# A second split of the input blocks, unscaled gate and up products, and another order of high parts, in a hybrid decoder step

## The chip, the cores and the metric

The kernel runs on one core of a Trainium2 chip. The metric is the device time of one execution in microseconds (us). A core has TensorE for matrix products (PE in the profile, and PEld for the loading of the stationary operand), VectorE (DVE), ScalarE (ACT), GpSimd (POOL) and SyncE (SP), which here only issues transfers. Each engine takes its instructions in the order in which they are written, and they wait for one another by semaphores.

## The reference

One layer of a decoder for 256 prompt positions and 8 sample tokens, together T = 264 columns: a half-step SwiGLU, a mixing block of four mLSTM heads beside a gated short convolution, another half-step SwiGLU, and a last RMSNorm. What matters here:

```python
def swiglu(x, wg, wu, wd):
    return (jax.nn.silu(x @ wg) * (x @ wu)) @ wd
h = h + 0.5 * swiglu(rmsnorm(h, norm_ffn1[l]), ffn1_gate[l], ffn1_up[l], ffn1_down[l])
mix, ... = mixing_block(rmsnorm(h, norm_mix[l]), w_in[l], ..., w_out[l], ...)
h = h + mix
h = h + 0.5 * swiglu(rmsnorm(h, norm_ffn2[l]), ffn2_gate[l], ffn2_up[l], ffn2_down[l])
```

D_MODEL is 2048, D_FF 5504; everything is float32. `rmsnorm` multiplies each token by the reciprocal root of its mean square, and each channel by a gain.

## The kernel before

**Data.** Channels lie on partitions, the 264 tokens in the free dimension. 2048 channels are 16 blocks of 128; D_FF is 43 blocks, taken in two halves of 22 and 21 (blocks 0 to 21, then 22 to 42). For each half all gate and up products are made, then the down products of that half for the 16 output blocks, which are added to the residual `h`.

**Three float16 products for a float32 one.** Each float32 operand is split into a high and a low float16 part. For weights ScalarE makes the high part (`high`, L246: a scaled copy) and VectorE the low one (`low`, L254: scaled source less high part). A block product is then three matmuls, high by high, high by low and low by high (`three`, L364 to L366); the third one of a weight tile is the first that needs VectorE's low part.

**Pairs.** For some blocks ("pairs") the gate and up products, or two down products, are made together by a seven-product scheme (`product_pair`): 264-column matmuls for the high parts (L438) and 132-column matmuls for the corrections (L423, L424). It needs sums of weight parts (`weight_sums`, L339, L342, L343, on VectorE), sums of token halves (`token_sums`, L411, made once for the input of an FFN and once for every eight blocks of activations), and a join of the results (`join`, one copy on ScalarE at L476 and six operations on VectorE, L479 to L486). A block that is no pair is called plain here.

**The norm.** The RMSNorm's per-token factor is not known when the input blocks are split (the sum of squares is still being made), so the split takes the bare `h` times the gain, and every gate and up product is multiplied by the factor `norm.r` afterwards: L895 for a pair, L914 and L920 for a plain block. Then follow Silu (ScalarE), the product of the two (L863), and the split of the activation into parts (L246 and L254 again, tiles `a`).

**Weights.** `weight_plan` lists the weight tiles in their order of use; `fetch` takes the next one: SyncE issues the transfer into one of three float32 buffers (`wraw`), ScalarE makes the high part in one of four buffers (`w`), VectorE the low part, and for a tile of a pair the sums. A tile holds 16 blocks of 128 x 128 (1 MB); a pair's gate and up are two tiles of 8 + 8. Three tiles are kept ahead of the product in work (`AHEAD`). In the FFNs the low part is put off (`held`, `lag`): `fetch` is called in the middle of a product, and the low part is written at the start of the next one (`release`).

**Order.** The order on each engine is that in which the Python code runs. Work that belongs beside the products is put on an agenda: `at(n, f)` runs f at the n-th following `tick`; each product makes a full tick at its start and half a tick in its middle. The activation work of a block so runs in the ticks of the next blocks' products. All VectorE and ScalarE instructions of one tick stand in their queues before what follows in the code, the next low part for one.

**Check and second pass.** The kernel checks that sums of its products lie in bounds, and if one doesn't, a branch runs the whole step again in a float32 form. That code stands in the program and isn't executed otherwise.

## Time and profile before

| | |
|---|---|
| time, median of 3 runs | 1855.82 us (1854.87 to 1857.45) |
| profiled execution | 1855.79 us, span 1854.1 us |
| TensorE busy | 1790.9 us, 97% |
| VectorE busy | 1617.1 us, 87% |
| ScalarE busy | 864.8 us, 47% |
| read from memory | 366.72 MB |

The stages on the profile's time axis: FFN 1 from the start to about 712 us (its second half's gate and up products between about 373 and 590), the mixing block to about 1140, FFN 2 to the end. A row of the waits says which engine, tile and line waited for which, with the total, the number and the longest; a row of the timeline gives start, duration, engine, line and tiles, and in brackets how long the engine stood before it and for whom. A matmul's duration is its passage through the array; matmuls overlap, so what one costs is read from the distance of starts.

### The profile page before, as it was taken

How to read it: one execution, taken by the hardware profiler on the slowest of the kernel's cores; microseconds unless marked ns; L12 is line 12 of the kernel's file. 1: busy time of each engine (PE TensorE's matmuls, PEld its weight loads, DVE VectorE, ACT ScalarE, POOL GpSimd, SP SyncE). 2: the span in 40 equal slices, each digit the busy share in tenths (PEclk: the TensorE clock that was granted, in tenths of full speed). 3: DMA queues.
4: the chain of work that ended last, by engine and by line, in shares of the span. 5: the costliest groups of instructions: out<-in, count | busy, mean ns of one | idle time of the engine just before them, and what ended most of it. 6: DMA issues, size and time to landing. Idle time of an engine off the chain costs nothing.

```text
span 1854.1 us, 44580 instructions
## 1 busy us (share of the span) xinstructions
PE 1790.9 (97%) x19596; PEld 1600.9 (86%) x19596; DVE 1617.1 (87%) x2196; ACT 864.8 (47%) x1216; POOL 160.1 (9%) x200
## 2 busy tenths in 40 slices
PE   9999999989999999999999999999999999999997
PEld 7889988979988987888888888998888987988886
DVE  7899989999997898788887866999989999999785
ACT  7534443334444435466566644444443434444442
POOL 1000000000000222322121021000000000000241
PEclk9999999999999999999999999999999999999999
DMA  8555555555555556878777655555565655555653
GB/s 299 197 183 203 186 195 190 193 198 189 205 206 169 185 165 224 290 257 300 275 248 259 215 202 172 196 186 204 182 209 172 213 198 195 198 186 188 197 176 125
DMA packets 90794, 381.45 MB, mean 206 GB/s; under 512 B 9788, under 2 KB 19612, under 8 KB 71392
## 3 DMA queue, kind: packets, MB, share of 16 engines
q1 hardware_dynamic: 81392, 350.51, 55.4%
q0 software_dynamic: 8256, 27.57, 4.4%
q8 instruction: 155, 2.54, 0.6%
q10 hardware_dynamic: 944, 0.45, 0.1%
q14 instruction: 47, 0.39, 0.1%
HBM read 366.72 MB, written 11.78 MB: 204 GB/s over the span
## 4 chain that ended last, share of the span: by engine, by line
DVE 47%; PE 39%; issue 6%; ACT 4%; DMA 4%; POOL 1%; SPq 0%; DVEq 0%; ACTq 0%; POOLq 0%
DVE w L254 20%; PE ps L366 11%; PE ps L364 11%; PE ps L365 11%; DVE s L339 8%; DVE s L342 4%; ACT w L246 2%; DVE s L343 2%; PE ps L438 2%; PE ps L424 2%; PE ps L423 2%; DMA wraw<-in_w1d 1%; DVE y L895 1%; DVE y L480 1%; DVE a L254 1%
## 5 line engine op out<-in xcount | busy, mean ns | idle before, releaser
L254 DVE SCALAR_TENSOR_TENSOR w<-wraw,w 128x2048 f16<-128x2048 f32 (+3 forms) x351 | 753.5, 2151 | 86.3 <-ACT w L246 86.1
L246 ACT ACTIVATE w<-wraw 128x2048 f16<-128x2048 f32 (+3 forms) x351 | 620.1, 1780 | 197.2 <-DMA wraw<-in_w1d 66.3
L366 PE MATMUL ps<-x,w 128*128 128x264 f16 x1280 | 358.0, 280 | 28.5 <-DVE w L254 28.4
L366 PEld LDWEIGHTS <-w 128*128 128x128 f16 x3028 | 297.9, 98 | 85.6 <-DVE w L254 40.6
L364 PE MATMUL ps<-x,w 128*128 128x264 f16 x1280 | 357.8, 280 | 0.0
L365 PE MATMUL ps<-x,w 128*128 128x264 f16 x1280 | 357.6, 279 | 0.0
L365 PEld LDWEIGHTS <-w 128*128 128x128 f16 x3028 | 298.1, 98 | 46.7
L364 PEld LDWEIGHTS <-w 128*128 128x128 f16 x3028 | 298.2, 98 | 45.3 <-issue 0.6
L364 PE MATMUL ps<-xm,w 128*128 128x264 f16 x896 | 248.1, 277 | 0.0
L366 PE MATMUL ps<-xm,w 128*128 128x264 f16 x896 | 248.1, 277 | 0.0
L365 PE MATMUL ps<-xm,w 128*128 128x264 f16 x896 | 248.1, 277 | 0.0
L438 PEld LDWEIGHTS <-w 128*128 128x128 f16 x2230 | 213.8, 98 | 29.7
L424 PEld LDWEIGHTS <-s 128*128 128x128 f16 x2216 | 215.1, 97 | 0.0
L423 PEld LDWEIGHTS <-s 128*128 128x128 f16 x2216 | 213.1, 96 | 1.8 <-DVE s L343 1.1
L339 DVE TENSOR_TENSOR s<-w 128x2048 f16<-128x2048 f16 (+2 forms) x145 | 173.1, 1194 | 7.7
L424 PEld LDWEIGHTS <-w 128*128 128x128 f16 x1676 | 163.2, 97 | 12.3 <-DVE w L254 10.0
L438 PE MATMUL ps<-x,w 128*128 128x264 f16 x1408 | 172.8, 276 | 0.0
L423 PEld LDWEIGHTS <-w 128*128 128x128 f16 x1676 | 163.2, 97 | 2.3
L366 PE MATMUL ps<-a,w 128*128 128x264 f16 (+2 forms) x596 | 156.8, 270 | 5.7 <-DVE w L254 5.7
L364 PE MATMUL ps<-a,w 128*128 128x264 f16 (+2 forms) x596 | 156.7, 270 | 0.0
L365 PE MATMUL ps<-a,w 128*128 128x264 f16 (+2 forms) x596 | 156.7, 269 | 0.0
L423 PE MATMUL ps<-f,s 128*128 128x132 f16 x1056 | 130.8, 220 | 0.0
(276 smaller groups left out, 2582.1 us busy)
## 6 DMA issues: line engine op xcount, KB each, us to landing
wraw<-in_w2gu SPq DMA_DIRECT2D x86, 1024.0 KB, 5.1
wraw<-in_w1gu SPq DMA_DIRECT2D x82, 1024.0 KB, 5.2
wraw<-in_win SPq DMA_DIRECT2D x56, 1024.0 KB, 5.7
wraw<-in_w1d SPq DMA_DIRECT2D x20, 1024.0 KB, 5.0
wraw<-in_w2d SPq DMA_DIRECT2D x18, 1024.0 KB, 5.0
wraw<-in_wout SPq DMA_DIRECT2D x16, 1024.0 KB, 4.8
wraw<-in_w2d SPq DMA_DIRECT2D x18, 704.0 KB, 4.1
wraw<-in_w1d SPq DMA_DIRECT2D x16, 704.0 KB, 4.1
```

The source lines that it names most:

```text
L246: nc.scalar.activation(dst, src, AF.Copy, scale=scale)
L254: nc.vector.scalar_tensor_tensor(dst, src, scale, hi, op0=ALU.mult, op1=ALU.subtract)
L339: nc.vector.tensor_tensor(s[:, 0:2], bc, d_.unsqueeze(1).to_broadcast([128, 2, m, 2, 128]), op=ALU.add)
L342: nc.vector.tensor_tensor(s[:, 2], s[:, 1], b_, op=ALU.add)
L343: nc.vector.tensor_tensor(s[:, 3], s[:, 2], a_, op=ALU.add)
L364: nc.tensor.matmul(ps, wh, xk[:, 0, :], start=first, stop=False)
L365: nc.tensor.matmul(ps, wh, xk[:, 1, :], start=False, stop=False)
L366: nc.tensor.matmul(ps, wl, xk[:, 0, :], start=False, stop=last)
L423: nc.tensor.matmul(ps, w[0], x[:, 1], start=first, stop=False)
L424: nc.tensor.matmul(ps, w[1], x[:, 0], start=False, stop=last)
L438: nc.tensor.matmul(ps[:, :T], hi[:, i], xs[i][:, 0], start=(k0 + i == 0), stop=False)
L480: nc.vector.tensor_tensor(y[:, 1:3], p[:, 1:3], y[:, 4].unsqueeze(1).to_broadcast([128, 2, TH]), op=ALU.add)
```

## The change

- **Blocks split a second time.** Once `norm.r` is known, `renew` multiplies each of the 16 input blocks by gain and norm (L820 in the new numbering) and splits the result again (L249 on ScalarE, L257 on VectorE), two blocks at each half tick, over four products (blocks 3 and 4 of FFN 1, 1 and 2 of FFN 2). From block 5 (FFN 1) or 3 (FFN 2) on, the products use the new blocks (`swap`), whose token sums (`form`) are made after that.
- **Products unscaled.** From there on a product needs no multiplication by the norm: Silu reads it with a constant scale, for a plain block directly from PSUM (L950), and the product of gate and up takes the scale along (L899).
- **High parts in front.** In gate, up and down products the next tile is fetched at the product's start, ahead of the activations on the agenda for that tick, and its low part is written in the middle of the same product.
- **Small pieces in the mixing.** The weight tiles of the mixing's projections are fetched in halves of 8 blocks (512 KB), each split on its own; lookahead is counted in halves (`AHEAD` 6).
- **Pairs.** 45 gate and up pairs instead of 44, spread more evenly (never three in a row), and 17 down pairs instead of 19.
- The join has its own buffer in two copies.

```diff
+def spread(b0, b1, n):
+    return [b0 + i for i in range(b1 - b0) if (i + 1) * n // (b1 - b0) > i * n // (b1 - b0)]
 GU_SEVEN = {
-    n: [b0 + i for b0, b1 in ((first, 21), (22, NFB - 1)) for i in range(b1 - b0) if i % 5 in (0, 2, 3)]
-    for n, first in (("1", 7), ("2", 3))
+    "1": spread(7, 21, 9) + spread(22, NFB - 1, 13), "2": spread(4, 21, 10) + spread(22, NFB - 1, 13),
 }
 DOWN_SEVEN = {
-    ("1", 0): (1, 2, 3, 5, 6, 7), ("1", 1): (1, 3, 4, 6),
-    ("2", 0): (1, 2, 3, 5, 6, 7), ("2", 1): (1, 3, 4),
+    ("1", 0): (1, 3, 4, 6, 7), ("1", 1): (1, 3, 4, 6),
+    ("2", 0): (1, 3, 4, 6, 7), ("2", 1): (1, 3, 4),
 }
...
     def add(key, src, n, m=128):
-        parts = -(-n // (WIDE if sevens else WK))
+        halves = sevens and key[0] in ("in", "out")
+        parts = -(-n // (WIDE if sevens and not halves else WK))
...
-    AHEAD = 3 if half_size else 2
+    AHEAD = 6 if half_size else 2
...
+    def product_wide(key, x, order, final):
+        ps, k = bank()[:, :T], 0
+        count = len(order)
+        while k < count:
+            while room() or not ready:
+                fetch()
+            hi, lo, n = take(key)
+            if room() and not (final and k):
+                fetch()
+            if k == 0:
+                tick()
+                middle = n if n < count else n // 2
+            for i in range(n):
+                three(ps, hi[:, i], lo[:, i], x[order[k]], k == 0, k == count - 1)
+                k += 1
+                if k == middle:
+                    release()
+                    tick(0.5)
+                    middle = 0
+            release()
+        return ps
...
     def product_pair(key, x, forms, order):
-        tick()
...
         while k0 < count:
-            while plan and len(ready) + len(held) < AHEAD or not ready:
+            while room() or not ready:
                 fetch()
-            got, hi, lo, n = ready.pop(0)
-            assert got == key, (got, key)
-            release()
+            hi, lo, n = take(key)
+            if room():
+                fetch()
+            if k0 in (0, WK):
+                tick()
             s = sums.pop(0)
...
-            fetch()
+            release()
             if last or k0 == 0:
                 tick(0.5)
...
-            if k0 == n:
-                tick()
...
+        def renew(self, *blocks):
+            for kb in blocks:
+                g, i = kb // WK, kb % WK
...
+                t, x = t264("sq"), self.new[g][:, i]
+                gain = whole[:, self.col + kb : self.col + kb + 1]
+                nc.vector.scalar_tensor_tensor(t, h[kb], gain, self.r, op0=ALU.mult, op1=ALU.mult)
+                split(x, t, 1.0)
+        def swap(self):
+            self.groups, self.scaled = self.new, True
+            self.x = [t[:, i] for t in self.new for i in range(WK)]
...
+                    nc.vector.scalar_tensor_tensor(
+                        zu, src, unit, sg, op0=ALU.mult, op1=ALU.mult
+                    )
...
                 def halves():
                     rest()
-                    nc.vector.tensor_tensor(
-                        z, z, norm.r.unsqueeze(1).to_broadcast([128, 2, T]), op=ALU.mult
-                    )
-                    nc.scalar.activation(sg, z[:, 0], AF.Silu)
+                    nc.scalar.activation(sg, z[:, 0], AF.Silu, scale=unit)
...
+                    if norm.scaled:
+                        sg = t264("tb")
+                        nc.scalar.activation(sg, pg, AF.Silu, scale=unit)
+                        watch(pg, scalar=True)
+                        pu = gate_up(j, "u")
+                        activated(j, i, t264("tc"), sg, pu)
+                        watch(pu, scalar=True)
+                        return
...
+                    if half_size and j == (5 if start is not None else 3):
+                        norm.swap()
...
                     if half_size and j == (3 if start is not None else 1):
+                        for n in range(WK):
+                            at(1 + n / 2, norm.renew, 2 * n, 2 * n + 1)
                         for g in range(2):
-                            at((4 + 2 * g) if start is not None else (1 + g), norm.form, g)
+                            at(6 + g + (start is not None), norm.form, g)
```

How the order moves is shown at three places. First VectorE in FFN 1, around the end of a plain block that stands behind a pair and in front of one; `w` are weight tiles, `s` their sums, `tc` the product of gate and up, `a1` the activation's parts. Before:

```order
L920 TENSOR_TENSOR tc_2251<-ps_2198,rstd_621 128x264
L863 TENSOR_TENSOR tc_2251<-tc_2251,tb_2189 128x264
L254 SCALAR_TENSOR_TENSOR w_2224<-wraw_2223,w_2224 128x16x128
L339 TENSOR_TENSOR s_2261<-w_2224 128x2048
L342 TENSOR_TENSOR s_2261<-s_2261,w_2224 128x1024
L343 TENSOR_TENSOR s_2261<-s_2261,w_2224 128x1024
L254 SCALAR_TENSOR_TENSOR a1_1469<-y5_2116,a1_1469 128x264
L254 SCALAR_TENSOR_TENSOR a1_1469<-tc_2251,a1_1469 128x264
L254 SCALAR_TENSOR_TENSOR w_2282<-wraw_2281,w_2282 128x16x128
```

With the change, at the like place:

```order
L899 SCALAR_TENSOR_TENSOR tc_2131<-ps_2071,tb_2067 128x264
L257 SCALAR_TENSOR_TENSOR w_2140<-wraw_2139,w_2140 128x16x128
L360 TENSOR_TENSOR s_2160<-w_2140 128x2048
L363 TENSOR_TENSOR s_2160<-s_2160,w_2140 128x1024
L364 TENSOR_TENSOR s_2160<-s_2160,w_2140 128x1024
L257 SCALAR_TENSOR_TENSOR a1_1600<-y4_1997,a1_1600 128x264
L257 SCALAR_TENSOR_TENSOR a1_1600<-tc_2131,a1_1600 128x264
L257 SCALAR_TENSOR_TENSOR w_2223<-wraw_2222,w_2223 128x16x128
```

The multiplication by the norm is gone; behind the activation's product stands, as before, a low part, but of another tile, as the second place shows: ScalarE at the same stretch (`seen` is the bounds check's read). Before:

```order
L246 ACTIVATE a1_1469<-y5_2116 128x264
L246 ACTIVATE w_2224<-wraw_2223 128x16x128
L246 ACTIVATE a1_1469<-tc_2251 128x264
L647 ACTIVATE seen_2255,stat_172<-ps_2198 128x16
L246 ACTIVATE w_2282<-wraw_2281 128x16x128
L246 ACTIVATE w_2365<-wraw_2364 128x16x128
```

With the change:

```order
L249 ACTIVATE w_2073<-wraw_2072 128x16x128
L249 ACTIVATE a1_1600<-y4_1997 128x264
L249 ACTIVATE a1_1600<-tc_2131 128x264
L658 ACTIVATE seen_2134,stat_173<-ps_2071 128x16
L249 ACTIVATE w_2140<-wraw_2139 128x16x128
L249 ACTIVATE w_2223<-wraw_2222 128x16x128
```

The tile whose low part VectorE makes right behind the activation's product (w_2224, now w_2140) had its high part ahead of that activation's split; now it has it behind. Third, VectorE in FFN 2, where input blocks are split again; `sq` is a block times gain and norm, `r0` its new parts:

```order
L820 SCALAR_TENSOR_TENSOR sq_15845<-h0_80,whole_166,rstd_15727 128x264
L257 SCALAR_TENSOR_TENSOR r0_15811<-sq_15845,r0_15811 128x264
L820 SCALAR_TENSOR_TENSOR sq_15849<-h0_80,whole_166,rstd_15727 128x264
L257 SCALAR_TENSOR_TENSOR r0_15811<-sq_15849,r0_15811 128x264
L957 TENSOR_TENSOR ta_15877<-ps_15804,rstd_15727 128x264
L820 SCALAR_TENSOR_TENSOR sq_15888<-h4_81,whole_166,rstd_15727 128x264
L257 SCALAR_TENSOR_TENSOR r0_15811<-sq_15888,r0_15811 128x264
L820 SCALAR_TENSOR_TENSOR sq_15892<-h4_81,whole_166,rstd_15727 128x264
L257 SCALAR_TENSOR_TENSOR r0_15811<-sq_15892,r0_15811 128x264
L257 SCALAR_TENSOR_TENSOR w_15885<-wraw_15884,w_15885 128x16x128
```

Between two of VectorE's rows of one block lies ScalarE's high part of it; the high part of w_15885 stands on ScalarE ahead of those of h4's two blocks:

```order
L658 ACTIVATE seen_15879,stat_173<-ps_15804 128x16
L960 ACTIVATE tb_15881<-ta_15877 128x264
L249 ACTIVATE w_15885<-wraw_15884 128x16x128
L249 ACTIVATE r0_15811<-sq_15888 128x264
L249 ACTIVATE r0_15811<-sq_15892 128x264
```

Four low parts of weight tiles stand among the sixteen blocks in this way. In all the program issues 74 more weight transfers, and TensorE has 112 more matmuls of 264 columns and 196 fewer of 132.

More of the change, by code (lines that the diff above doesn't have):

```diff
@@ L135, in weight_plan @@
     half = KB // 2
-    if sevens:
-        beside(("two", 0), a["wout"][0:2], KB)
-    else:
-        for k0 in (0, half):
-            for db in range(2):
-                add(("out", db), a["wout"][db][:, k0 : k0 + half], half)
+    for k0 in (0, half):
+        for db in range(2):
+            src = a["wout"][db][:, k0 : k0 + half]
+            plan.append((("out", db), src, half, 128, 1, db if sevens else None))
     for db in range(2, KB):
@@ L263, in fetch @@
             return
-        key, src, n, m, several = plan.pop(0)
+        key, src, n, m, several, sub = plan.pop(0)
         if half_size and key == "four":
             raw, parts = small()
+        elif half_size and sub == 1:
+            raw, parts = (t[:, WK:] for t in pair)
         elif half_size:
@@ L269, in fetch @@
             parts = wpool.tile([128, WIDE, 2, 128], PART, tag="w", name="w", bufs=4)
+            pair[:] = raw, parts
             raw = raw[:, :, :m]
@@ L298, in fetch, with size, room, take @@
         release()
-        held.append((lows, (key, parts[:, :, 0], parts[:, :, 1], n), parts))
+        held.append((lows, (key, parts[:, :, 0], parts[:, :, 1], n, size(key, sub)), parts))
         if not lag[0]:
             release()
-    held, lag = [], [False]
+    held, lag, pair = [], [False], []
+    def size(key, sub):
+        return 0 if key == "four" else 2 if half_size and sub is None else 1
+    def room():
+        if not plan:
+            return False
+        asked = sum(t[4] for t in ready) + sum(t[1][4] for t in held)
+        return asked + size(plan[0][0], plan[0][5]) <= AHEAD
+    def take(key):
+        got, hi, lo, n, _ = ready.pop(0)
+        assert got == key, (got, key)
+        return hi, lo, n
     def release():
@@ L496, in product_beside @@
         ps = bank()[:, :T]
-        while plan and len(ready) + len(held) < AHEAD:
+        while room() or not ready:
             fetch()
-        got, hi, lo, n = ready.pop(0)
-        assert got == key and n == KB, (got, key, n)
+        hi, lo, n = take(key)
         for k in range(0, n, 4):
@@ L542, in products2 @@
             for j, key in enumerate(keys):
-                while plan and len(ready) + len(held) < AHEAD:
+                while room() or not ready:
                     fetch()
-                got, hi, lo, n = ready.pop(0)
-                assert got == key, (got, key)
+                hi, lo, n = take(key)
                 for i in range(n):
@@ L551, in products2 @@
                     )
-                fetch()
+                if room():
+                    fetch()
                 if j == 0:
@@ L604, in products4 @@
                     squares(i, i + 1)
-            _, hi, lo, _ = ready.pop(0)
+            hi, lo, _ = take("four")
             for n, (w, part) in enumerate(((hi, 0), (hi, 1), (lo, 0))):
@@ L872, in activated @@
                 if lag[0] and j < blocks[-1] - 2:
-                    at(0.5 if j in sevens and j + 1 in sevens else 1.5, low, *rest)
+                    at(1.5, low, *rest)
                 else:
```

103 lines of the change are left out of this document (42 added, 61 removed).

## The prediction

> **What bounds the kernel now.** I read the page's first part, then who TensorE waited for, then the stages, then VectorE's own order of time at the longest wait.
>
> ```profile
> span 1854.1 us, 44580 instructions
> PE 1790.9 (97%) x19596; PEld 1600.9 (86%) x19596; DVE 1617.1 (87%) x2196; ACT 864.8 (47%) x1216; POOL 160.1 (9%) x200
> ```
>
> TensorE leaves 63.2 us of the span. The waits of TensorE say whom it waited for (total, times, longest):
>
> ```profile
> PE ps L366 <- DVE w L254: 34.1, 21, 4.0
> PE ps L424 <- DVE w L254: 7.5, 8, 1.6
> ```
>
> So 41.6 us are the third matmul of a block, which needs the low part of a weight tile, waiting for VectorE (L254). By stages (columns: PE, PEld, DVE, ACT, POOL busy, clock, DMA share, GB/s):
>
> ```profile
> 365.00:605.00 240.00, 229.85 (x2660) 206.89 (x2658) 222.12 (x283) 103.86 (x140) 0.63 (x1) 0.99 0.57 195
> 712.00:1150.00 438.00, 431.64 (x3745) 372.55 (x3734) 335.86 (x581) 253.27 (x404) 89.33 (x132) 1.00 0.70 246
> ```
>
> In the second half of FFN 1 (365 to 605) VectorE has no room: 222 of 240 us, and the same waits there, and VectorE's own for the tiles' high parts (365 to 590), are
>
> ```profile
> PE ps L366 <- DVE w L254: 9.7, 5, 4.0
> PE ps L424 <- DVE w L254: 0.4, 1, 0.4
> ```
> ```profile
> L254 DVE SCALAR_TENSOR_TENSOR w<-wraw,w 128x2048 f16<-128x2048 f32 (+1 forms) x42 | 95.1, 2266 | 1.4 <-ACT w L246 1.4
> ```
>
> In the mixing (712 to 1150) it has 100 us of it, and no TensorE wait there names a weight tile. At the longest wait VectorE is back to back (first fence), and TensorE stands for 4 us (second):
>
> ```profile
> 400.56 2.28 DVE L254 SCALAR_TENSOR_TENSOR w<-wraw,w 128x2048 f16<-128x2048 f32 x1
> 402.94 1.23 DVE L339 TENSOR_TENSOR s<-w 128x2048 f16<-128x2048 f16 x1
> 404.20 0.69 DVE L342 TENSOR_TENSOR s<-s,w 128x1024 f16<-128x1024 f16 x1
> 404.93 0.69 DVE L343 TENSOR_TENSOR s<-s,w 128x1024 f16<-128x1024 f16 x1
> 405.54 0.28 DVE L479 TENSOR_TENSOR y<-y,ps 128x132 f32<-128x132 f32 x1
> ...
> 407.56 0.71 DVE L895 TENSOR_TENSOR y<-y,rstd 128x528 f32<-128x528 f32 x1
> 408.18 2.28 DVE L254 SCALAR_TENSOR_TENSOR w<-wraw,w 128x2048 f16<-128x2048 f32 x1
> 410.38 0.43 DVE L863 TENSOR_TENSOR y<-y,tb 128x264 f32<-128x264 f32 x1
> 410.73 2.29 DVE L254 SCALAR_TENSOR_TENSOR w<-wraw,w 128x2048 f16<-128x2048 f32 x1
> ```
> ```profile
> 410.52 0.29 PE L366 MATMUL ps<-x,w 128*128 128x264 f16 x1 [3.99 <-DVE w L254]
> ```
>
> The starts give prices on a loaded VectorE: a low part with its sums 4.98 (400.56 to 405.54), a low part alone 2.20, the join 2.02 (405.54 to 407.56), the product with the norm 0.62, a small operation 0.35. TensorE's prices:
>
> ```profile
> 1147.20:1168.80 21.60, 21.60 (x194) 18.77 (x193) 16.14 (x23) 10.77 (x18) 0.00 (x0) 1.00 0.38 120
> ```
> ```profile
> 385.18 1.96 PE L438 MATMUL ps<-x,w 128*128 128x264 f16 x16
> ...
> 390.19 0.39 PE L438 MATMUL ps<-x,w 128*128 128x264 f16 x2
> ```
>
> Four plain products take 21.60, so a plain block (gate and up) 10.80; half a pair 5.01, a pair 10.02. A pair costs VectorE 2 x 4.98 + 2.02 + 0.62 + 2 x 0.35 = 13.30, a plain block 2 x 2.20 + 4 x 0.38 = 5.9. Twelve pairs and 8 plain blocks with 7 for the token sums are 214 against 207 on TensorE: 7 short, and 10.1 are waited in that window. This account of VectorE therefore fits, and I use it for the change.
>
> **The change, part by part.** TensorE: 112 more matmuls of 264 columns and 196 fewer of 132. At 21.60/192 = 0.1125 and (5.01 - 16 x 0.1125)/56 = 0.0573 that is 12.6 - 11.2 = **+1.3 us**.
>
> Norm product gone: a pair costs VectorE 12.68, a plain block after the switch 2 x 2.20 + 2 x 0.38 = 5.2. Over 45 pairs and 33 plain blocks that is 28 + 23 = 51 us off its work, and two fewer down pairs take off about 2 x 9 more.
>
> But two things are put in front of its low parts. First, **the place of the high part**. Before, the tile fetched in the middle of the up product had its high part ahead of that block's activation; now the tile's high part stands behind it on ScalarE, and VectorE's next instruction after the activation product is this tile's low part (the two rows of VectorE's order shown above, L899 and then L257). The chain is in the trace:
>
> ```profile
> 1156.32 0.43 DVE L863 TENSOR_TENSOR tc<-tc,tb 128x264 f32<-128x264 f32 x1
> ```
> ```profile
> 1156.84 0.42 ACT L246 ACTIVATE a<-tc 128x264 f16<-128x264 f32 x1 [3.22 <-issue]
> 1157.16 0.17 ACT L647 ACTIVATE seen<-ps 128x16 f32<-128x16 f32 x1
> 1157.23 0.19 ACT L647 ACTIVATION_READ_ACCUMULATOR seen<-ps 128x1 f32 x1
> 1157.32 1.90 ACT L246 ACTIVATE w<-wraw 128x2048 f16<-128x2048 f32 x1
> ```
>
> From the product's end (1156.75) to the high part's end (1159.22) are 2.5 us in which VectorE, being in order, does nothing. A VectorE that is early doesn't mind; a late one pays 2.5 per plain block, so 7.7 instead of 5.2. Bounds: 0 and 2.5; I take 2.5, because a plain block and two pairs cost VectorE 5.2 + 25.4 = 30.6 against 30.8 on TensorE even without it: any wait makes it late. With it: 33.1 against 30.8. Thirteen pairs and 7 plain blocks are 165 + 54 + 7 = 226 against 206, 20 short. The fetch is half a product earlier than before, and by walking one cycle through the order its tightest tile is ready 6 us early; take that off, and a little for fewer pairs in a row ahead of it: **12.5 us** of waiting where 10.1 are now.
>
> Second, **the second split** (L820 and the two splitting operations): 16 blocks in each FFN, each VectorE, ScalarE, VectorE in turn. The same pattern before:
>
> ```profile
> 1141.51 0.43 DVE L1697 SCALAR_TENSOR_TENSOR h<-ps,h 128x264 f32<-128x264 f32 x1 [0.29 <-PE ps L366]
> 1142.53 0.49 DVE L254 SCALAR_TENSOR_TENSOR x<-h,gains,x 128x264 f16<-128x264 f32 x1 [0.58 <-ACT x L246]
> 1142.94 0.17 DVE L651 TENSOR_REDUCE stat<-ps 128x1 f32<-128x16 f32 x1
> ```
>
> 1.43 per block, or 1.33 with a constant scale: 21 us. Of the four blocks that share a product, the first two have a weight tile's high part ahead of them on ScalarE (third order fence): 2 more, four times: 8. All this falls into four products, 21.6 on TensorE, in which VectorE also has four low parts and some 8 small operations (12): 41 against 21.6. Walking FFN 2 with these prices from 1158.3 (where the old token sums start), the low parts of products 3 up, 4 gate and 4 up come 4.5, 4.7 and 3.2 late, the next few 2 to 3 together: **15 us**. In FFN 1 VectorE is already hard up where this begins,
>
> ```profile
> 54.43 2.28 DVE L254 SCALAR_TENSOR_TENSOR w<-wraw,w 128x2048 f16<-128x2048 f32 x1
> ```
>
> the tile done at 56.7 for a product that starts at 57.8: **18 us**. Bounds: 0 if the splits ran in VectorE's idle time, 24 with no lead at all. What is late next is the rest of the first halves, now entered without lead: 9 pairs and 4 plain blocks in FFN 1 (145 + 5 against 133, less the 6 that plain blocks 5 to 7 give back, **11**), 9 and 6 in FFN 2 (160 + 5 against 155, less 1, **9**).
>
> Down products and start: the waits now, in the down products that end FFN 1 (605 to 712) and in the first 100 us,
>
> ```profile
> PE ps L366 <- DVE w L254: 2.1, 1, 2.1
> PE ps L424 <- DVE w L254: 1.6, 1, 1.6
> ```
> ```profile
> PE ps L366 <- DVE w L254: 1.9, 1, 1.9
> ```
>
> The second-half down products keep their pairs: 3 each, **6**. The first halves lose their three pairs in a row: 0. The start keeps its **1.9**. Mixing: 72 tiles in two pieces; VectorE and ScalarE have the room (window above), SyncE's 74 more issues are free. Without that cover it would be a fixed part per piece, under 0.2 each, 14 us.
>
> The sum against the profiled run (1855.79, span 1854.1, 1.7 around it; median 1855.82, so no shift): waits for weight tiles 1.9 + 18 + 15 + 11 + 9 + 2 x 12.5 + 6 = 86 in place of 41.6, +1.3: 1855.8 + 44 + 1.3 = **1901 us**.
>
> A row for a cost beyond the wait itself, the granted clock after the 4 us wait:
>
> ```profile
> 411.00:416.00 5.00, 5.00 (x32) 3.65 (x30) 4.47 (x9) 2.34 (x3) 0.00 (x0) 0.66 0.83 282
> 416.00:421.00 5.00, 5.00 (x47) 4.34 (x46) 4.90 (x5) 2.22 (x2) 0.00 (x0) 1.00 0.62 198
> ```
>
> Fifteen matmuls fewer, about 1.7 us. While VectorE is the late one, this gives it time and costs nothing more, so it isn't in the sum. The Trainium skill, "TensorE: Matmul & The Clock Gate" (HAM oscillation), says that idle gaps above about 3.4 us bring the clock back to half; the trace agrees (0.66 in that window). By that rule alone, some six to eight such gaps would add 10 to 14 us, an estimate, and give about 1913.
>
> **The rivals.**
>
> *Faster, the waits go.* VectorE has 69 us less to do, and 32 x 0.86 = 28 more from the splits; if the waits on ScalarE fell into time in which it waits for TensorE anyhow, all but about 7 of the 41.6 would go, and with them four slow-clock stretches of 1.7: 1855.8 - 35 - 7 + 1.3 = 1815. For it: the fetch is half a product earlier, pairs never stand three in a row. Against it: the order of rows shown, and 30.6 against 30.8 without any wait.
>
> *No change.* The 2.5 is hidden, but the splits are paid: 1.9 + 18 + 15 + 5 = 40 for 41.6: 1855.
>
> *Slower by the transfers.* The mixing's 72 tiles come as two transfers. Issues and their time to landing:
>
> ```profile
> wraw<-in_w2d SPq DMA_DIRECT2D x18, 1024.0 KB, 5.0
> ...
> wraw<-in_w2d SPq DMA_DIRECT2D x18, 704.0 KB, 4.1
> ...
> raw<-in_w1gu SPq DMA_DIRECT2D x16, 256.0 KB, 5.7
> ```
> ```profile
> 0.00:25.00 25.00, 22.60 (x197) 19.42 (x198) 18.73 (x42) 17.77 (x33) 2.43 (x11) 1.00 0.96 318
> ```
>
> At 3.6 a half (estimate: 4.1 less 192 KB at the slope of the two upper rows), one after the other, 7.2 against the 5.4 that a product lasts: 72 x 1.8 = 130, 2030 with the rest. Against it: the 256 KB pieces at the start overlap and reach 318 GB/s. [...]
>
> **How the numbers follow.** Forecast 66%, faster 21%, no change 9%, transfers 4%. The forecast's own range is 1878 to 1922 (the wait terms off by a quarter, all one way). Reaching to the no-change case and a little of the faster one, and leaving the transfers out, 8 in 10 lie in **1846 to 1922**. A measurement here tells 0.2% (3.7 us) from no change: faster 0.22, same 0.08, slower 0.70.
>
> **What would show it.** Right: TensorE's waits for VectorE's low part (now L257) at 70 to 100 us in all; VectorE's waits for ScalarE's high part in the FFNs, near 2.5 us at each plain block behind a pair, where the second half of FFN 1 has 1.4 in all; waits of 3 to 6 us near 63 to 85 us and soon after FFN 2 begins; none in the mixing. Wrong: VectorE on time in the second halves, or its splits overlapping. If the unscaled products left the bounds that the kernel checks, its second, float32 pass would run and the time would more than double; I give that under 1%.

## The result and the profile after

The changed kernel takes 1912.37 us (1910.23 to 1917.14, 4 runs) where the kernel before takes 1856.51 us (the median of four runs beside it): a ratio of 1.0305, 95% interval 1.0284 to 1.0327. It is 3% slower, 56 us in the medians. The profiled executions are 1917.14 us, the longest of the four, and 1855.79 us, with spans of 1915.4 and 1854.1 us, so the profiles have 61.3 us to explain.

The first part of the page of the changed kernel:

```profile
span 1915.4 us, 44686 instructions
PE 1809.5 (94%) x19512; PEld 1605.0 (84%) x19512; DVE 1574.6 (82%) x2207; ACT 878.9 (46%) x1325; POOL 144.8 (8%) x200
```

VectorE has 42.5 us less to do than before (1617.1), as the change intends, and the kernel is longer. TensorE's waits, whole run (total, times, longest):

```profile
PE ps L387 <- DVE w L257: 50.7, 25, 4.7
PE ps L385 <- ACT r L249: 23.3, 16, 3.2
PE ps L474 <- ACT w L249: 7.2, 6, 1.8
PE ps L385 <- ACT w L249: 3.6, 3, 1.8
PE ps L458 <- DVE w L257: 3.1, 8, 0.8
```

These rows are 87.9 us; the two rows of before were 41.6. L387 and L458 are the old waits for a low part of a weight tile. The second row is new in kind: `r` are the input blocks split a second time, and TensorE waits for them one by one. The third and fourth are waits for a high part. And VectorE's largest wait, whole run, before and after:

```profile
DVE w L254 <- ACT w L246: 86.1, 59, 4.2
```
```profile
DVE w L257 <- ACT w L249: 189.4, 110, 3.9
```

In the order of the change VectorE, about to write a tile's low part, finds ScalarE's high part not there 110 times, in place of 59. Before, 63.6 of the 86.1 us lay in the mixing, where VectorE has time to spare; now 34.8 of the 189.4 do.

The stages, each from the first matmul of its kind to the first of the next kind (read from TensorE's rows of the two traces, us):

| stage | before | after | difference |
|---|---|---|---|
| start and first half gate and up, FFN 1 | 246.4 | 270.6 | +24.2 |
| down, first half | 116.4 | 118.3 | +1.9 |
| gate and up, second half | 232.4 | 231.9 | -0.5 |
| down, second half | 115.8 | 122.4 | +6.6 |
| mixing | 430.4 | 424.1 | -6.3 |
| first half gate and up, FFN 2 | 233.3 | 255.5 | +22.2 |
| down, first half | 117.1 | 118.1 | +1.0 |
| gate and up, second half | 233.2 | 232.8 | -0.4 |
| down, second half, and end | 129.2 | 141.7 | +12.5 |

Three quarters of the loss lie where the blocks are split a second time. There VectorE's and TensorE's order of time are these (FFN 1, `sq` a block times gain and norm, `r` its new parts):

```profile
85.71 0.43 DVE L257 SCALAR_TENSOR_TENSOR r<-sq,r 128x264 f16<-128x264 f32 x1 [2.42 <-ACT r L249]
86.06 0.49 DVE L820 SCALAR_TENSOR_TENSOR sq<-h,whole,rstd 128x264 f32<-128x264 f32 x1
87.04 0.43 DVE L257 SCALAR_TENSOR_TENSOR r<-sq,r 128x264 f16<-128x264 f32 x1 [0.49 <-ACT r L249]
87.39 2.28 DVE L257 SCALAR_TENSOR_TENSOR w<-wraw,w 128x2048 f16<-128x2048 f32 x1
```
```profile
85.73 0.38 PE L385 MATMUL ps<-r,w 128*128 128x264 f16 x1 [3.22 <-ACT r L249]
...
87.06 0.38 PE L385 MATMUL ps<-r,w 128*128 128x264 f16 x1 [0.26 <-ACT r L249]
...
90.58 0.38 PE L385 MATMUL ps<-r,w 128*128 128x264 f16 x1 [2.46 <-ACT r L249]
```

From one low part to the next, 85.71 to 87.04, are the 1.33 us that the prediction worked with. In front of the first stands the wait of 2.42 us behind a tile's high part. TensorE has already begun the product that uses the new blocks and goes at the pace of the split, three matmuls at a time. The last of the splits comes long after the product that needs them has begun: 28.5 us in FFN 1 (63.4 to 91.9) and 22.5 us in FFN 2 (1200.2 to 1222.7), where such a product takes 5.4 without waits.

In the second half of FFN 1 the place of the high part shows as forecast, VectorE first, ScalarE second:

```profile
409.02 0.43 DVE L899 SCALAR_TENSOR_TENSOR tc<-ps,tb 128x264 f32<-128x264 f32 x1
411.90 2.29 DVE L257 SCALAR_TENSOR_TENSOR w<-wraw,w 128x2048 f16<-128x2048 f32 x1 [2.45 <-ACT w L249]
```
```profile
409.48 0.42 ACT L249 ACTIVATE a<-tc 128x264 f16<-128x264 f32 x1 [5.84 <-DVE tc L899]
...
409.97 3.70 ACT L249 ACTIVATE w<-wraw 128x2048 f16<-128x2048 f32 x2
```

ScalarE stood still for 5.84 us, nearly all of it with the tile's data there (they had landed at 404.1), because the activation's split, which waits for the product's end, is in front of the high part.

### The profile page after: what moved, and what is told of

It reads as the page before. It is cut to its first block, busy times and chain, and to the rows that moved or that the text cites. A ratio compares the mean times of both kernels' runs of the same rounds, so it can differ in the third digit from the quotient of the medians.

```text
span 1915.4 us, 44686 instructions
## 1 busy us (share of the span) xinstructions
PE 1809.5 (94%) x19512; PEld 1605.0 (84%) x19512; DVE 1574.6 (82%) x2207; ACT 878.9 (46%) x1325; POOL 144.8 (8%) x200
## 5 line engine op out<-in xcount | busy, mean ns | idle before, releaser
L257 DVE SCALAR_TENSOR_TENSOR w<-wraw,w 128x2048 f16<-128x2048 f32 (+4 forms) x425 | 756.3, 1797 | 189.7 <-ACT w L249 189.4
L249 ACT ACTIVATE w<-wraw 128x2048 f16<-128x2048 f32 (+4 forms) x425 | 628.2, 1505 | 153.8 <-DMA wraw<-in_w1d 38.0
L387 PEld LDWEIGHTS <-w 128*128 128x128 f16 x3084 | 304.8, 99 | 110.7 <-DVE w L257 58.0
L387 PE MATMUL ps<-r,w 128*128 128x264 f16 x1056 | 299.3, 283 | 31.6 <-DVE w L257 31.6
L385 PE MATMUL ps<-r,w 128*128 128x264 f16 x1056 | 298.7, 283 | 23.3 <-ACT r L249 23.3
L386 PE MATMUL ps<-r,w 128*128 128x264 f16 x1056 | 298.4, 283 | 1.6 <-DVE r L257 0.2
L387 PE MATMUL ps<-xm,w 128*128 128x264 f16 x896 | 247.3, 276 | 0.0
L458 PEld LDWEIGHTS <-s 128*128 128x128 f16 x2160 | 209.6, 97 | 0.0
L457 PEld LDWEIGHTS <-s 128*128 128x128 f16 x2160 | 207.7, 96 | 0.5
L387 PE MATMUL ps<-a,w 128*128 128x264 f16 (+2 forms) x684 | 183.2, 274 | 17.2 <-DVE w L257 17.1
L385 PE MATMUL ps<-a,w 128*128 128x264 f16 (+2 forms) x684 | 183.3, 274 | 3.6 <-ACT w L249 3.6
L386 PE MATMUL ps<-a,w 128*128 128x264 f16 (+2 forms) x684 | 183.1, 273 | 0.0
L474 PE MATMUL ps<-r,w 128*128 128x264 f16 x1440 | 176.8, 276 | 3.4 <-ACT w L249 3.4
L360 DVE TENSOR_TENSOR s<-w 128x2048 f16<-128x2048 f16 (+1 forms) x141 | 166.3, 1180 | 7.5
L458 PEld LDWEIGHTS <-w 128*128 128x128 f16 x1634 | 159.2, 98 | 8.5 <-DVE w L257 6.4
```

Source lines behind the costliest of these rows:

```text
L249: nc.scalar.activation(dst, src, AF.Copy, scale=scale)
L257: nc.vector.scalar_tensor_tensor(dst, src, scale, hi, op0=ALU.mult, op1=ALU.subtract)
L360: nc.vector.tensor_tensor(s[:, 0:2], bc, d_.unsqueeze(1).to_broadcast([128, 2, m, 2, 128]), op=ALU.add)
L385: nc.tensor.matmul(ps, wh, xk[:, 0, :], start=first, stop=False)
L386: nc.tensor.matmul(ps, wh, xk[:, 1, :], start=False, stop=False)
L387: nc.tensor.matmul(ps, wl, xk[:, 0, :], start=False, stop=last)
```

## The experiments

All are edits of the changed kernel or of one another, timed beside the kernel before, four at a time; the expectations were written with the results of the earlier runs known.

### The place of the fetch undone

In gate, up and down products and in pairs the next tile is fetched in the middle again, and its low part comes at the start of the next product.

```diff
             hi, lo, n = take(key)
-            if room() and not (final and k):
+            if final and k == 0 and room():
                 fetch()
             if k == 0:
                 tick()
+                release()
...
+                if not final and room() and k == (n // 2 if n == count else k) and (
+                    n == count or i == n - 1
+                ):
+                    fetch()
                 if k == middle:
-                    release()
                     tick(0.5)
                     middle = 0
-            release()
...
-            if room():
-                fetch()
             if k0 in (0, WK):
                 tick()
+            release()
...
-            release()
+            if room():
+                fetch()
             if last or k0 == 0:
```

> The changed kernel, with the place of the fetch as before (in gate, up and down products and in pairs the next tile is fetched in the middle, its low part written at the start of the following product). Theory (high parts that stand behind ScalarE's reads of a finished product hold VectorE up): VectorE's waits for ScalarE's high parts in the second half of FFN 1 go from 19 us to under 6, TensorE's waits for low parts there from 10 to about 4; the last down products get back most of the 12 us by which they are longer than before the change (142 to about 130 us), the down products that end FFN 1 about 5; the second split keeps its 38 us. In all 1912 - 6 - 6 - 12 - 5 - 4 = about 1879 us. Rival (VectorE's amount of work sets the waits, the order doesn't): waits move but the sum stays, 1905 to 1915.

Measured: 1834.57 us, 0.9892 of the kernel before (0.9875 to 0.9908). One place in the code turns 3% slower into 1% faster; it is worth 78 us, more than twice what I expected. VectorE's wait for high parts in the second half of FFN 1, first the changed kernel, then this one, and what TensorE waits for in this one there:

```profile
DVE w L257 <- ACT w L249: 17.2, 7, 2.5
```
```profile
DVE w L257 <- ACT w L249: 0.9, 1, 0.9
```
```profile
PE ps L387 <- DVE w L257: 0.4, 1, 0.4
```

The stage falls from 231.9 to 217.5 us, where I had left 4 us of waiting. The same rows of VectorE and ScalarE as above, in this kernel:

```profile
406.54 0.43 DVE L902 SCALAR_TENSOR_TENSOR tc<-ps,tb 128x264 f32<-128x264 f32 x1
406.88 2.28 DVE L257 SCALAR_TENSOR_TENSOR w<-wraw,w 128x2048 f16<-128x2048 f32 x1
```
```profile
402.07 1.90 ACT L249 ACTIVATE w<-wraw 128x2048 f16<-128x2048 f32 x1
407.00 0.42 ACT L249 ACTIVATE a<-tc 128x264 f16<-128x264 f32 x1 [3.03 <-DVE tc L902]
```

The high part is ready three microseconds ahead, and the low part follows the activation's product at once. The last down stage goes from 141.7 to 128.6 us, and the two first-half stages get back 11.3 and 12.8 us; VectorE's waits inside the splits fall from 26.5 to 17.2 us. I had left the first halves' loss untouched. Of the 82 us between the two spans, 57 are TensorE's waits for tiles and new blocks (87.9 to 30.9), and an estimated 17 are the slower clock behind such waits (worked out below with the granted clock).

### Only the activation moved behind the next high part

```diff
                         pu = gate_up(j, "u")
-                        activated(j, i, t264("tc"), sg, pu)
-                        watch(pu, scalar=True)
+
+                        def up_done():
+                            activated(j, i, t264("tc"), sg, pu)
+                            watch(pu, scalar=True)
+
+                        up_done() if i == len(blocks) - 1 else at(1, up_done)
                         return
```

> The changed kernel, with the activation of an unscaled plain block put on the agenda of the next product's start, so that on ScalarE the next tile's high part stands ahead of the activation's split; fetch and low parts stay where the change has them, and the down products too. Theory: the same gain as from the earlier place in the gate and up products alone, about 6 us in each second half and 4 in the first halves, none in the down products: about 1896 us. Rival (amount of work): 1912.

Measured: 1878.04 us, ratio 1.0123 (1.0106 to 1.014): 34 us back where I expected 16. In the second half of FFN 1 VectorE's wait and TensorE's are now

```profile
DVE w L257 <- ACT w L249: 0.3, 1, 0.3
```
```profile
PE ps L387 <- DVE w L257: 4.0, 1, 4.0
```

Here fetch and low part stand where the change has them; what is new is that on ScalarE the next tile's high part stands ahead of the activation's split. So in the gate and up products it is this order that holds VectorE up, not the earlier fetch. The down products kept theirs, and the last stage is still 136.9 us.

### The second split in two stages

```diff
                 nc.vector.scalar_tensor_tensor(t, h[kb], gain, self.r, op0=ALU.mult, op1=ALU.mult)
-                split(x, t, 1.0)
+                high(x[:, 0, :], t, 1.0)
+                self.due.append((x[:, 1, :], t, x[:, 0, :], 1.0))
+            for parts in due:
+                low(*parts)
...
+                        at(1 + WK / 2, norm.renew)
```

(`due` holds the low parts of the step before.)

> The changed kernel, with the second split written in two stages: a step makes the products with gain and norm and the high parts of two blocks, and the low parts of the two blocks of the step before; the amount of work is the same. Theory (the split is a chain VectorE, ScalarE, VectorE of 1.33 us a block and a high part of a tile in front of some): VectorE needs some 15 us for 16 blocks where it needs 29 with its waits, TensorE's 38 us of stalls in the two places fall to about 10: about 1885 us. Rival (VectorE is over its time there by the amount of work, and the debt comes out as waits for low parts of the following blocks): 1900 or more.

Measured: 1885.2 us, ratio 1.0174 (1.0152 to 1.0195), the time that the theory gave. Its terms were off: TensorE's waits at the two splits fall from 28.2 to 13.9 us, not from 38 to 10, and the last down stage, 136.9 for 141.7, gives some of the rest. VectorE's order is now without a wait between the instructions of a split:

```profile
63.65 0.89 DVE L825 SCALAR_TENSOR_TENSOR y<-h,whole,rstd 128x264 f32<-128x264 f32 x2
64.46 0.77 DVE L257 SCALAR_TENSOR_TENSOR r<-y,r 128x264 f16<-128x264 f32 x2
```

That is 1.5 us for two blocks instead of 2.66 and more, and the two first-half stages are 259.7 and 242.8 us for 270.6 and 255.5.

### The mixing in whole tiles

```diff
-        halves = sevens and key[0] in ("in", "out")
+        halves = False
```

> The changed kernel, with the tiles of the mixing's projections whole again (1 MB instead of two pieces of 512 KB), all else as changed. The stage of the mixing is 6 us shorter with the change (424 us for 430). If that comes from the pieces, the mixing is 430 again and the time 1918 us. If it comes from something else (the state in which it is entered, the last projection's order) 1912, and if pieces cost a fixed part each, 1900 to 1908.

Measured: 1913.04 us, ratio 1.0323 (1.0302 to 1.0343): no difference from the change. In its profile the mixing is 426.8 us, between the two, with

```profile
PE ps L387 <- DVE w L257: 3.0, 4, 1.8
```

where the pieces have no such row in that stage. But the kernel with the split in two stages, which has the pieces, takes 426.4 us in that stage too, so the runs show no gain from the pieces.

### Both effects apart: without the second split, and with both repairs

The kernel with the fetch in the middle, once with the products scaled by the norm as before, and once with the split in two stages.

```diff
-                        for n in range(WK):
-                            at(1 + n / 2, norm.renew, 2 * n, 2 * n + 1)
                         for g in range(2):
-                            at(6 + g + (start is not None), norm.form, g)
+                            at((4 + 2 * g) if start is not None else (1 + g), norm.form, g)
...
-                    if half_size and j == (5 if start is not None else 3):
-                        norm.swap()
...
-                    nc.scalar.activation(sg, z[:, 0], AF.Silu, scale=unit)
+                    nc.vector.tensor_tensor(
+                        z, z, norm.r.unsqueeze(1).to_broadcast([128, 2, T]), op=ALU.mult
+                    )
+                    nc.scalar.activation(sg, z[:, 0], AF.Silu)
```

> The kernel with the fetch in the middle, without the second split: the products keep the first blocks and are multiplied by the norm as before the change, the token sums are made at once; pairs and pieces as changed. Theory (VectorE's work decides in the second halves once the order is right: by the prices of the prediction 13 pairs, 7 plain blocks and the token sums are 221 us with the norm's products and 208 without, TensorE 206): the second halves' stages go from 217.5 back to about 227 each, the first halves, with no second split, from 259 to 245 and from 243 to 234; in all about 1832 us, no gain and no loss within 6. Rival (order and spread of the pairs alone shorten the second halves): they stay at 218, and the time is about 1811 us, so that the second split would be loss only.

Measured: 1845.33 us, ratio 0.996 (0.9946 to 0.9975), where I expected 1832. The second halves are back at 231.5 and 233.0 us, and in that of FFN 1 TensorE waits

```profile
PE ps L387 <- DVE w L257: 10.2, 4, 4.0
```

So the second halves are short of VectorE when the products are scaled (221 us of work by the prediction's prices for 206 of TensorE) and when the order is wrong (226); with unscaled products in the right order (208) the stage is TensorE's own 217.5. The second halves get shorter only with both, unscaled products and the fetch in the middle. My expectation of 227 each was too low: 221 was enough for as much waiting as before the change.

> The kernel with the fetch in the middle, and the second split in two stages as in the run of that alone. Theory (two independent causes): the stalls left in the first halves, 19 and 9 us, lose another 8 and 7: about 1819 us. Rival (what the two-stage split saved was the wait for the tile's high part in front, which the earlier fetch has already moved away): at most 5 saved, about 1830 us.

Measured: 1814.22 us, ratio 0.9788 (0.9768 to 0.9808). The two repairs nearly add up (78 and 20 us; the second alone was 27).

### The second split at half the speed, and with GpSimd

One block at each half product instead of two; the second of the two leaves the product with the norm to GpSimd.

```diff
-                        for n in range(WK):
-                            at(1 + n / 2, norm.renew, 2 * n, 2 * n + 1)
+                        for n in range(KB):
+                            at(1 + n / 2, norm.renew, n)
+                        at(1 + WK, norm.renew)
...
-                    if half_size and j == (5 if start is not None else 3):
+                    if half_size and j == (7 if start is not None else 5):
...
-    "1": spread(7, 21, 9) + spread(22, NFB - 1, 13), "2": spread(4, 21, 10) + spread(22, NFB - 1, 13),
+    "1": spread(7, 21, 9) + spread(22, NFB - 1, 13), "2": spread(6, 21, 10) + spread(22, NFB - 1, 13),
```
```diff
-                nc.vector.scalar_tensor_tensor(t, h[kb], gain, self.r, op0=ALU.mult, op1=ALU.mult)
+                nc.gpsimd.tensor_tensor(t, h[kb], self.r, op=ALU.mult)
```

> The kernel with the fetch in the middle, and the second split in two stages at half the speed: one block at each half product over eight products, the new blocks in use from block 7 (FFN 1) or 5 (FFN 2), in FFN 2 the ten pairs between blocks 6 and 20. Theory (27 us of VectorE's work at the old prices in 21.6 us of TensorE's are too much at once, in 43 us they fit): the stalls of the first halves fall to the 6 or so that FFN 1 has at its start and about 2: 1834.6 - 13 - 8 = about 1814 us. Rival (VectorE has no lead left when the pairs begin, and the waits come later, in the rest of the first halves): 1822 to 1828.

> As the run with the second split at half the speed, but the product of block and norm is made by GpSimd, and the gain goes into ScalarE's and VectorE's split; VectorE has 16 operations of 0.43 us in each FFN instead of 32. Theory: where the slow split already fits into VectorE's time, the 7 us less are worth nothing: 1814 us, the same within 3. Rival (VectorE is still short in the first halves): up to 7 us less for each FFN, 1805; or GpSimd and VectorE hinder each other, and VectorE's operations there get longer than 2.3 us for a low part: over 1818.

Measured: 1808.39 us (0.9754, 0.9735 to 0.9774) and 1808.8 us (0.9759, 0.9739 to 0.9779). At half the speed no wait names `r` any more. The gain over the faster two-stage split lies in FFN 1, whose first half falls from 250.7 to 245.1 us; FFN 2's is 231.7 us in both, less than before the change (233.3). I had expected 1814. GpSimd's share adds nothing, as the theory said of a VectorE that is no longer short there. But it also takes less off VectorE than the 7 us that I counted: in FFN 2 the split costs VectorE 14.5 us without GpSimd and 11.3 with it, because the operations that are left get longer (last section).

### How many pairs, and where

Four variants: 14 pairs in each second half of the slow kernel; its second halves and first-half down products with the pair lists of before; three down pairs that are no neighbours in the second half of FFN 1; and that last one with GpSimd's product and one pair more in each first half.

```diff
-spread(22, NFB - 1, 13)
+spread(22, NFB - 1, 14)
```
```diff
-spread(22, NFB - 1, 13)
+[22 + i for i in range(20) if i % 5 in (0, 2, 3)]
...
-    ("1", 0): (1, 3, 4, 6, 7)
+    ("1", 0): (1, 2, 3, 5, 6, 7)
...
-    ("2", 0): (1, 3, 4, 6, 7)
+    ("2", 0): (1, 2, 3, 5, 6, 7)
```
```diff
-    ("1", 1): (1, 3, 4, 6)
+    ("1", 1): (1, 3, 6)
```
```diff
-spread(7, 21, 9)
+spread(7, 21, 10)
...
-spread(6, 21, 10)
+spread(6, 21, 11)
```

> The kernel of the slow second split (1808.4 us), with 14 pairs of 20 blocks in each second half where it has 13, spread evenly. Theory (a stage is as long as the larger of TensorE's and VectorE's work by the prices of the prediction): VectorE 14 x 12.68 + 6 x 5.2 + 7 = 216 us for 205 on TensorE, where 13 pairs are 208 for 206 and leave 0.6 us of stalls; 8 us of stalls in each second half against 0.8 saved: about 1822 us. Rival (VectorE's lead at entry and its gaps take it up): 1807, no loss.

Measured: 1818.97 us, ratio 0.9806 (0.979 to 0.9822): 10.6 us more than with 13. TensorE's waits in the second half of FFN 1:

```profile
PE ps L387 <- DVE w L257: 5.3, 2, 3.2
```

The account of VectorE said 216 for 205 and 8 us of stalls; it holds in sign, and to 3 us there. The longer of the two waits, 3.2 us, stands behind the second of two stretches of three pairs in a row, which the list of 13 doesn't have; so the amount of work and its order aren't told apart here.

> The kernel of the slow second split, with the pair lists of before in the second halves (12 pairs, up to three in a row) and in the down products of the first halves (six pairs, three in a row). Theory (with unscaled products VectorE has 201 us of work for 207 there, so that order and spread of the pairs don't matter): second halves without stalls and 0.8 us longer each, down products between 1 us shorter and 3 longer each, 1808 to 1815. Rival (three pairs in a row make VectorE late whatever its sum is): 4 to 5 us of stalls in each second half, as before the change 10, about 1820.

Measured: 1821.54 us, ratio 0.9822 (0.9806 to 0.9839), as the rival had it, though for another reason. The expectation calls the second halves' list three in a row; it has at most two, as the gate and up lists had before the change as well, and three stand in a row in the down products alone. With 201 us of work for 207, TensorE waits in the second half of FFN 1

```profile
PE ps L387 <- DVE w L257: 3.6, 2, 2.3
```

and both waits lie in its first 46 us, behind the down pairs 5, 6 and 7 and the pair of block 22 (four on end) and behind blocks 24 and 25; from 406 us to the end of the stage there is none. In each FFN the down stage in front is 2.4 or 2.6 us longer than in the slow kernel, and the second half 4.2. My reading is that four pairs on end use up VectorE's lead and that it takes some blocks to come back, so that what stands at a stage's entry counts beside its sum. The run changes the down lists and the second halves' lists together, so this isn't shown by itself.

> The kernel of the slow second split, with three down pairs that never stand next to each other, 1, 3 and 6, in the second half of FFN 1, where it has 1, 3, 4 and 6. Theory: the 4.5 us that TensorE waits at the second of the two neighbours and behind it go, one pair fewer costs 1.0: about 1805 us. Rival (the split of the mixing's input blocks makes VectorE late there, not the neighbours): the waits stay, 1809.

Measured: 1803.95 us, ratio 0.9722 (0.9706 to 0.9738). This is the fastest kernel of the study, 2.8% faster than before. TensorE's waits in that stage, first of the slow kernel, then of this one:

```profile
PE ps L461 <- DVE w L257: 2.4, 2, 2.1
PE ps L387 <- DVE w L257: 2.1, 1, 2.1
```
```profile
PE ps L461 <- DVE w L257: 0.3, 1, 0.3
```

The run takes away a pair and a neighbour at once, and in the last down stage of the slow kernel the same neighbours, 3 and 4, leave no wait for a low part at the second of them; so which of the two it is stays open.

> The kernel with the product of block and norm on GpSimd, with the three down pairs of the run beside it and one pair more in each first half (10 and 11). Theory: VectorE has 7 us fewer from GpSimd's share and 7.5 more from the pair, so the waits stay as they are and TensorE saves 0.8 twice: about 1803 us. Rival (VectorE has no room left): waits for low parts in the first halves, 1806 to 1812.

Measured: 1819.21 us, ratio 0.9808 (0.9792 to 0.9824), slower by 15 us than the run beside it. The first halves are 250.3 and 239.5 us; from 50 to 250 us TensorE waits

```profile
PE ps L387 <- DVE w L257: 6.5, 2, 3.2
PE ps L461 <- DVE w L257: 1.2, 1, 1.2
```

The prediction's prices would have told: 10 pairs and 4 plain blocks (7 to 20) are 147.6 us of VectorE's work for 143.4 on TensorE, 11 and 4 (6 to 20) are 160.3 for 153.4, 4 and 7 short; the stages are 5.7 and 7.8 us longer than with one pair fewer and GpSimd (244.6 and 231.7). What GpSimd takes over lies in the blocks of the split, ahead of the pairs, and is about 3 us for each FFN instead of 7.

The page of the fastest kernel begins

```profile
span 1801.7 us, 44476 instructions
PE 1775.8 (99%) x19452; PEld 1596.6 (89%) x19452; DVE 1572.8 (87%) x2202; ACT 886.2 (49%) x1329; POOL 154.5 (9%) x200
```

with VectorE's busy time as in the changed kernel (1574.6): the 108 us between the two come out of order and place, not of work.

## Why the prediction was right, and where it was off

**Direction, range and sum.** Forecast 1901 us, 1846 to 1922; measured 1912. The waits for weight tiles and new blocks were to be 86 us and are 87.9; TensorE's work was to grow by 1.3.

| term of the sum | forecast | measured wait |
|---|---|---|
| start | 1.9 | 1.9 |
| second split, FFN 1 and 2 | 18 + 15 | 16.2 + 12.0 |
| rest of the first halves | 11 + 9 | 4.1 + 3.0 |
| second halves | 12.5 + 12.5 | 12.2 + 11.8 |
| down products | 0 + 6 | 6.3 + 20.5 |

That 86 and 87.9 lie so close is luck: single terms of the table are off by up to 15 us, in both directions.

**The place of the high part: right.** The 2.5 us that I took out of bounds 0 and 2.5 are 17.2 us in 7 waits, 2.46 each, at each plain block among the pairs of that stage. The two runs that take it away show that it is the cause.

**The second split: right in size, wrong in what waits.** I had walked VectorE's lateness into low parts of the following products. In FFN 1 one such wait came (4.7 us); the rest, and in FFN 2 all, is TensorE waiting for the new blocks, since the swap comes before the last of them are split. The step that failed is the one that named "the low parts of products 3 up, 4 gate and 4 up". So the sign that I gave, waits for VectorE's low part of 70 to 100 us in all, didn't come: they are 53.8 (50.7 + 3.1), and the other 34.1 name ScalarE. The rest of the first halves was to cost 20 us and costs 7; that VectorE enters it with more lead because TensorE was held up before is likely and wasn't tested. (For FFN 2 the sum also has a pair too few: 10 pairs and 6 plain blocks are left there, not 9 and 6, which by the same prices gives 12 and not 9.) The whole stages are +24.2 and +22.2 where my terms less the waits of before give +24.7 and +21.

**The down products: the term that was mis-sized.** I kept the waits of the second halves as before (3 each) and took those of the first (6.3 before) to go to 0. They are 26.7 in all. The place of the high part acts there too. VectorE and then ScalarE in the last stage of the changed kernel:

```profile
1887.95 0.43 DVE L1020 SCALAR_TENSOR_TENSOR h<-ps,h 128x264 f32<-128x264 f32 x1
1891.09 1.62 DVE L257 SCALAR_TENSOR_TENSOR w<-wraw,w 128x1408 f16<-128x1408 f32 x1 [2.71 <-ACT w L249]
```
```profile
1889.12 0.52 ACT L1067 ACTIVATE h<-h,vecs 128x264 f32<-128x264 f32 x1 [2.98 <-POOL sq L830]
...
1889.69 1.36 ACT L249 ACTIVATE w<-wraw 128x1408 f16<-128x1408 f32 x1
```

VectorE adds the product to `h`, GpSimd squares it, ScalarE scales it, reads the product (two short rows left out), and only then makes the high part for which VectorE stands. In that stage VectorE waits as follows, in the changed kernel and in the one with the fetch in the middle:

```profile
DVE w L257 <- ACT w L249: 31.6, 14, 3.6
```
```profile
DVE w L257 <- ACT w L249: 9.3, 6, 2.5
```

I had looked for this chain in the plain gate and up blocks alone. This error, 21 us, and those of the second split and the first halves, 5 and 13 the other way, nearly cancel in the sum.

**The granted clock: left out wrongly.** I said that its cost gives VectorE time and isn't in the sum. Of the span's 61.3 us, the waits explain 87.9 - 41.6 = 46.3 and the work 1.3; 13.7 are left. Around the second split of FFN 2 (columns as in the prediction's windows):

```profile
1202.00:1206.00 4.00, 1.21 (x10) 0.77 (x8) 1.62 (x4) 2.69 (x6) 0.00 (x0) 1.00 0.58 233
...
1210.00:1214.00 4.00, 1.96 (x6) 0.71 (x6) 3.02 (x8) 1.02 (x4) 0.00 (x0) 0.50 0.56 177
...
1222.00:1226.00 4.00, 3.64 (x16) 2.18 (x16) 1.45 (x4) 2.41 (x5) 0.00 (x0) 0.50 0.67 240
1226.00:1230.00 4.00, 4.00 (x35) 3.33 (x33) 3.57 (x4) 2.64 (x5) 0.00 (x0) 0.91 0.13 23
```

When the waits are over, shortly before 1223, TensorE works 4 us more at half the clock: 16 matmuls where the next 4 us have 35, some 2 us lost with nothing to wait for. Over the whole run the granted clock is 0.50 for 76 us in the changed kernel and for 27 before, up to the last matmul; without TensorE's waits these are 53 and 24, of which half is lost: 26 and 12, an estimate from the two traces. These 14 us more, less 4 by which TensorE's other waits got shorter, make 10 of the 13.7; the rest stays open. The mean granted clock is 0.978 in the changed kernel, 0.990 before and 0.998 in the fastest one.

The Trainium skill, "TensorE: Matmul & The Clock Gate" (HAM oscillation), which the prediction cited for about 1913 us, comes out nearer than my sum, and the measured 0.50 agrees with it. But that nearness is luck too: the prediction counted six to eight gaps above 3.4 us, and there are three (4.7, 4.0 and 3.9). The clock also fell behind shorter waits here (last section), and there the measurement decides.

**The mixing** was to stay and got 6.3 us shorter. Of this 4.7 are TensorE's waits for small results inside it, 6.4 before and 1.7 after, the largest before 2.4 us (L1228, for `gl`). With whole tiles that one is gone as well; what made it go wasn't tried. The rival of halved transfers is excluded: whole tiles take the same time to within 1 us. A piece is on its way for as long as a whole tile was (first before, then after):

```profile
wraw<-in_win SPq DMA_DIRECT2D x56, 1024.0 KB, 5.7
```
```profile
wraw<-in_win SPq DMA_DIRECT2D x112, 512.0 KB, 5.7
```

but the pieces overlap, which my price of one after the other left out: at the 247 GB/s that the mixing moves in the changed kernel, 1.4 MB come in during 5.7 us, more than two pieces.

**The rival "faster, the waits go"** (1815) failed for this change and describes the repaired one: with the high parts ahead of the reads and the split in two stages the time is 1814. That the two numbers agree is partly luck, since 17.5 us of the waits for tiles and blocks are left there and not 7. What I held against it, VectorE's order of rows, was the reason. "30.6 against 30.8 without any wait" was no argument: at that balance the second halves run without waits (0.4 us).

## What to carry to other kernels

An instruction that waits for the end of a product must not stand on an in-order engine ahead of work for the next product whose result a third engine needs: list, for each engine, what stands behind the waiting instruction, in every stage that has the pattern. Work removed from an engine was worth nothing here while a wait in its queue was as large; and a chain that goes back and forth between two engines is cheap once its steps are written one step apart. And in these runs a balance of two engines over a whole stage was not enough: waits came behind stretches of three or four pairs.

## What was not expected of the hardware

The granted clock fell to 0.50 (windows above) behind a wait of 3.15 us and stayed there over 16 us of waits of 2.5 to 2.9 us with groups of six matmuls between them; until TensorE had been busy for nearly 4 us on end it did not rise. The length of one wait alone didn't decide it: the clock also fell behind waits of 2.63 us (345 us) and 2.03 us (0.51 from 1411 to 1414.5 us), and stayed at 1.00 behind one of 3.11 us (392.4 us). The first two of the waits in FFN 2, TensorE in order of time:

```profile
1206.45 0.38 PE L385 MATMUL ps<-r,w 128*128 128x264 f16 x1 [3.15 <-ACT r L249]
...
1211.30 0.38 PE L385 MATMUL ps<-r,w 128*128 128x264 f16 x1 [2.46 <-ACT r L249]
```

GpSimd's product of block and norm took 1.64 us where its addition of the same size takes 0.96 in the changed kernel. VectorE's low parts of weight tiles beside it kept their 2.28 (9 of them, mean 2281 ns), but its splits of the blocks took 0.72 us, where the same operation, with a gain as third operand, takes 0.49 (L254 `x<-h,gains,x` in the prediction) and the split without a gain 0.43. Why wasn't tried. First the addition, then the product and the splits from 55 to 100 us in the run with GpSimd:

```profile
L834 POOL TENSOR_TENSOR acc<-acc,sq 128x264 f32<-128x264 f32 x43 | 41.3, 961 | 3.4
```
```profile
L831 POOL TENSOR_TENSOR sq<-h,rstd 128x264 f32<-128x264 f32 x16 | 26.2, 1640 | 22.7 <-DVE rstd L758 8.0 <-ACT a L249 7.9 <-DVE r L257 6.9
```
```profile
L257 DVE SCALAR_TENSOR_TENSOR r<-sq,whole,r 128x264 f16<-128x264 f32 x16 | 11.5, 716 | 0.7 <-ACT r L249 0.7
```
